# Product five read from its PSUM bank, ones products read a unit later, and distances counted in streamed columns, in an encoder block on one core

## The chip, the cores and the metric

The kernel runs on one core of a Trainium2 chip. The metric is the device time of one launch in microseconds, lower is better. Names of the engines: PE is TensorE's matmul (PEld its weight load), DVE is VectorE, ACT is ScalarE, POOL is GpSimd, SP is SyncE, which issues the DMAs.

## What is computed

One layer of a hybrid encoder block on x of 1024 tokens by 1024 channels, float32:

```python
u = rms_norm(x, norm1_g)
q, k, v, cB, cC, cH, gates = split(u @ w_in)            # 512 each, gates 2048
A = neighbourhood_attention(q, k, v, rpb)               # 8 heads of 64
B = cB * conv3(cC * cH)
m = sigmoid(gA) * (A @ w_attn_branch) + sigmoid(gB) * (B @ w_conv_branch)
x = x + m @ w_o
x = x + square(relu(rms_norm(x, norm2_g) @ w_mlp_in)) @ w_mlp_out   # 1024 -> 4096 -> 1024
```

## The kernel before

**Arithmetic.** Every float32 operand of a product is scaled by a power of two and split into a high and a low float16 half. A product then runs three passes on PE: high by high, high by low, low by high. The power of two comes from a sum of squares (or a maximum) over the weights. Each partition's share is written into a column next to a tile of ones, a matmul with the ones ("ones product", `all_sum`, line 177) adds them over the partitions, DVE reads the result from PSUM (line 180), and `pow2_half` turns it into the scale (lines 401 to 408).

**Seven products.** The gate projection, W1 and W2 use a seven-product scheme for 2 x 2 blocks (`seven`, line 993). Of each weight group two blocks and four sums of blocks are formed. Each product is a *unit* (line 183): 12 matmuls of 512 columns, four row tiles by three passes, into one PSUM bank. The order in W1 is 1, 6, 5, 4, 2, 7, 3; in the gates it is 1, 6, 2, 4, 5, 7, 3. After a unit has been issued, the *post* of the unit before it runs: it reads PSUM and combines products. There are eight PSUM banks that are handed out in turn (`anybank`, line 74), so a bank that is read late holds up the unit that wants it next.

**Posts of W1** (`quad`, line 1282). Product 1 is copied by ACT, products 6 and 2 are added to it by DVE. `post5` (line 1292) copies product 5 to SBUF on ACT (L1293) and subtracts on DVE (L1294). `post7` (line 1296) makes three sums (L1297 to L1299); L1299 uses the copy of product 5. `post3` (L1302) adds product 3 and starts `h_done` (line 1265): ACT's ReLU (L1267) and its square with a sum (L1269), POOL's four sums (L1136), and the store of the seven forms to DRAM (L1273).

**How the work interleaves.** Every engine works its queue in the order in which the program issues it. The program has a foreground list `fg` and a background list `bg` of generators; `unit` lets each of them advance a fixed number of steps (2 and 5 in W1) after its matmuls. `apart(mark, n)` (line 159) keeps a generator waiting until n units have been issued since the mark. So the distance between the issue of a sum and of the ones product that reads it is written in units, whatever their size.

**Weight groups of W1.** There are 16 groups q; group q is used by quad q. `sums1(q)` (line 1190) scales the rows (`rows_scaled`, L941, ACT, eight pieces), takes the sums of squares (`forms_sum`, L950, ACT) and the four sums of blocks (L955, POOL), and adds the two partial sums (`sum_of`, L921 and L922, DVE). `prep1(q)` (line 1204) waits in `gate(q)` until quad q-3 is issued, calls `scale_of` (line 925: the distance, the ones product, the power of two), splits the seven forms with ACT (L974) and DVE (L968) in `forms_split`, and goes on to `sums1(q+1)`. The operands of three groups can be in SBUF at a time. The sums of blocks stand in `tsum`, two groups to a tile of the pool "ws".

**The gates** use the same helpers in `prep_s` (line 978) and `gate_units` (line 1016), where product 5 is copied by ACT as well (line 1047) and read by lines 1031 and 1032. **The projections** (Q, K, conv) get their scale in `Chunk.prep`, through the same `all_sum`; their splits are L287 (ACT) and L275 (DVE), and at the start of the kernel they share the engines with the forms of the tokens (L477 POOL, L479 and L471 ACT, L481 DVE).

**From W1 to W2.** `first2` is put on the background list behind `prep1(15)`: it loads four tiles of W2 (`w2x`) and the first of the stored forms. `prep2(s)` (line 1346) takes squares of W2 (L1359, ACT), `sum_of`, `scale_of`, and then splits activations (L1383 ACT, L1385 DVE) and weights (L1388 ACT, L1392 DVE) for each product; POOL makes the next weight sums (L1398, L1399). Quads 14 and 15 run beside this, then the 28 products of W2.

Of the kernel before, what the change touches and what calls it, by code (L numbers as in the profile page):

```python
# [14 lines left out]
AF = mybir.ActivationFunctionType  # L15
OP = mybir.AluOpType
# [36 lines left out]
def encoder_block(ctx: ExitStack, tc: tile.TileContext, x, weights, cols, gqk, rel, masks, out):  # L53
# [12 lines left out]
    def bank(tag):  # L66
        return psum.tile([128, 512], F32, name="ps_" + tag, tag=tag, bufs=banks[tag])
# [6 lines left out]
    def anybank():  # L74
        rc[0] += 1
        return bank("dsodsods"[rc[0] % 8])
# [78 lines left out]
        forced[0] = False  # L155

    late, units, forced, side = [], [0], [False], [False]

    def apart(mark, n=3):
        while units[0] < mark + n and not forced[0]:  # L160
            yield WAIT

    def built(*chs):
# [10 lines left out]
        turn[0] = (turn[0] + 1) % 4  # L174
        return ones[:, 128 + turn[0]:129 + turn[0]]

    def all_sum(a, out, bk, floor):
        T.matmul(bk[:, 0:1], ones[:, 0:128], a, start=True, stop=True)
        yield
        V.tensor_scalar(sc[:, out], bk[:, 0:1], floor, None, op0=OP.max)  # L180
        yield

    def unit(mms, post=None, steps=0, ticks=0):

        for ps, l, r, a, b in mms:
            T.matmul(ps, l, r, start=a, stop=b)  # L186
        units[0] += 1
        settle()
        if post:
            late.append(post)  # L190
        for i in range(max(steps, ticks)):
            if i < steps:
                step()
            if i < ticks:
                tick()

    def settle():
        while late:
            late.pop(0)()
# [17 lines left out]
    class Chunk:  # L217
# [75 lines left out]
        def largest(self, rm, a, b):  # L293
            o = 0
            for p, (k, w) in enumerate(self.widths):
                while len(self.raw) <= p:
                    yield WAIT
                V.tensor_reduce(sc[:, at(rm, o, k)], self.raw[p][:, :k * w].rearrange("p (k w) -> p k w", k=k),
                                axis=AX, op=OP.max, apply_absolute_value=True)
                o += k  # L300
                yield
            while not self.ready:
                yield WAIT
            mul(rm, self.rows, rm)
            yield
            V.tensor_reduce(sc[:, a], sc[:, rm], axis=AX, op=OP.max, apply_absolute_value=True)
            c = ones_col()
            V.tensor_copy(c, sc[:, a])
            if self.kind != "V":
                yield from apart(units[0], {"A": 3, "B": 3, "O": 1}[self.kind])  # L310
            yield from all_sum(c, b, bank(self.bank) if self.bank else anybank(), 1e-30)

    def push(*chunks):
        for ch in chunks:
# [226 lines left out]
    for p in range(11):  # L541
# [7 lines left out]
        for q in (p,) if p < 6 else (2 * p - 6, 2 * p - 5):  # L549
            c = q // 2 + 3  # L550
# [367 lines left out]
    def sum_of(sm):  # L918

        b, a = cols_of("prep", 1), ones_col()  # L920
        V.tensor_reduce(sc[:, b], sc[:, sm], axis=AX, op=OP.add)  # L921
        V.tensor_copy(a, sc[:, b])  # L922
        return a, units[0]

    def scale_of(am, more):

        a, mark = am
        yield from apart(mark)
        b, s, inv = cols_of("prep", 1), cols_of("prep", 1), keep()
        yield from all_sum(a, b, anybank(), 1e-36)  # L930
        yield from pow2_half(b, 14, s, inv, more)
        return s, inv
# [8 lines left out]
                A.activation(v, v, AF.Copy, scale=sc[:, at(g, 4 * i + k)])  # L941
            yield

    def forms_sum(ch, t):

        sm = cols_of("prep", 2)
        for i in range(2):
            while len(ch.raw) <= i:
                yield WAIT
            A.activation(t[:, 2:4].rearrange("p a c -> p (a c)"), ch.raw[i], AF.Square, accum_out=sc[:, at(sm, i)])  # L950
            yield
        ch.r = [ch.raw[i].rearrange("p (n m) -> p n m", n=2) for i in range(2)]
        (w11, w12), (w21, w22) = ([r[:, 0], r[:, 1]] for r in ch.r)
        for o, a, b in ((0, w11, w12), (1, w12, w22), (2, t[:, 0], w22), (3, t[:, 2], w21)):
            G.tensor_tensor(t[:, o], a, b, op=OP.add)  # L955
        yield
        ch.sum = sum_of(sm)
        yield

# [18 lines left out]
    def prep_s(n):  # L978

        ch = cS[n]  # L980
        t = w3p.tile([128, 4, 512], F32, name="gsum", bufs=1)
        yield from rows_scaled(ch, g1)
        yield from forms_sum(ch, t)
        s, ch.inv = yield from scale_of(ch.sum, 9)
        while done[0] < ch.first:
            yield WAIT
        ch.P = wsp.tile([128, 7, 2, 512], F16, name="w16_s", tag="ws")
        yield from forms_split(ch, t, s, ch.P)
        ch.split = True
# [26 lines left out]
    def gate_units(n, tail=None):  # L1016

        sg = w3p.tile([128, 4, 512], F32, name="sg")
        z = [sg[:, i] for i in range(4)]
        if n == 0:  # L1020
            for g in range(2):
                for half in range(2):
                    ps = anybank()
                    unit(ch_mms(ps, actU, half, cG, 8, 256, 128 * g),
                         lambda ps=ps, g=g, half=half: A.activation(z[2 * half + g], ps, AF.Sigmoid,
                                                                    scale=sc[:, cG.inv]), 3, 4)
            return sg

        def post7(ps):
            V.tensor_tensor(z[2], ps[7], z[1], op=OP.add)  # L1030
            V.tensor_tensor(z[1], z[3], z[1], op=OP.subtract)
            V.tensor_tensor(z[3], z[3], z[2], op=OP.subtract)
            V.tensor_tensor(z[2], ps[4], z[2], op=OP.add)
            if tail:
                A.activation(sg[:, 2:], sg[:, 2:], AF.Sigmoid, scale=sc[:, cS[n].inv])
                tail(sg, 1)

        def post3(ps):
            V.tensor_tensor(z[1], ps[3], z[1], op=OP.add)
            c = 2 if tail else 4  # L1040
            A.activation(sg[:, :c], sg[:, :c], AF.Sigmoid, scale=sc[:, cS[n].inv])
            if tail:
                tail(sg, 0)
        seven(cS[n].P, actS, 0, 512, {
            1: lambda ps: A.activation(z[0], ps[1], AF.Copy),
            6: lambda ps: V.tensor_tensor(z[1], ps[6], z[0], op=OP.add),
            5: lambda ps: A.activation(z[3], ps[5], AF.Copy),
            2: lambda ps: V.tensor_tensor(z[0], ps[2], z[0], op=OP.add),
            7: post7, 3: post3}, 2, 4 if n < 7 else 6, (1, 6, 2, 4, 5, 7, 3))
        return sg  # L1050

# [138 lines left out]
    def sums1(q):  # L1190

        ch = c1[q]
        while q == 2 and pair_done[0] < 4:
            yield
        if q == 0:
            tsum[0] = U2[1][:, 2].rearrange("p s k t -> p (s k t)").bitcast(F32).rearrange("p (i c) -> p i c", i=4)
        elif q == 1 or q % 2 == 0:
            t = wsp.tile([128, 2, 4, 512], F32, name="tsum", tag="ws")
            for i in range(2):
                tsum[q + i] = t[:, i]  # L1200
        yield from rows_scaled(ch, g2)
        yield from forms_sum(ch, tsum[q])

    def prep1(q):

        ch = c1[q]
        yield from gate(q)
        s, ch.inv = yield from scale_of(ch.sum, 9)
        pool, tag = TAGS[q % 3]
        P = P1[q] = pool.tile([128, 7, 2, 512], F16, name="w16_1", tag=tag)  # L1210
        yield from forms_split(ch, tsum[q], s, P)
        ready.add(q)
        if 0 < q < 15:
            yield from sums1(q + 1)
# [67 lines left out]
    def quad(q, c0=0, c1=512):  # L1282
        need(q)
        if c0 == 0:
            while q - 2 in live:
                step()
            live.add(q)
            AS[q] = w4p.tile([128, 7, 512], F32, name="as", tag="as")
        ps = {}
        z = [AS[q][:, i, c0:c1] for i in range(7)]  # L1290

        def post5(ps):
            A.activation(z[3], ps[5], AF.Copy)  # L1293
            V.tensor_tensor(z[1], z[3], z[5], op=OP.subtract)  # L1294

        def post7(ps):
            V.tensor_tensor(z[6], ps[7], z[5], op=OP.add)  # L1297
            V.tensor_tensor(z[2], ps[4], z[6], op=OP.add)  # L1298
            V.tensor_tensor(z[3], z[3], z[6], op=OP.subtract)  # L1299

        def post3(ps):
            V.tensor_tensor(z[1], ps[3], z[1], op=OP.add)  # L1302
            if c1 == 512:
                fg.append(h_done(q))
        seven(P1[q], actU2, c0, c1, {
            1: lambda ps: A.activation(z[4], ps[1], AF.Copy),
            6: lambda ps: V.tensor_tensor(z[5], ps[6], z[4], op=OP.add),
            5: post5,
            2: lambda ps: V.tensor_tensor(z[0], ps[2], z[4], op=OP.add),  # L1309
            7: post7, 3: post3}, 2, 5)  # L1310
# [251 lines left out]
```

## Time and profile before

| | before |
|---|---|
| median of 3 runs | 1300.35 us (1298.75 to 1300.73) |
| profiled execution, time | 1300.49 us |
| profiled execution, span | 1298.7 us |
| mean granted TensorE clock | 0.984 |
| DMA traffic | 173.35 MB, 133 GB/s over the span |

The profile is one execution with the time of every instruction. Lines like `839.94 1.92 ACT as L1267` give the start in microseconds, the duration, the engine, the tile and the line of the kernel. In the timeline a bracket such as `[4.23 <-DVE ones L922]` is the idle time of that engine before the instruction and what ended it. In a table by stage, the columns are the stretch, then the busy time and the count of instructions of PE, PEld, DVE, ACT and POOL, then the granted clock, the DMA share and GB/s. Groups of instructions read `line engine operation out<-in shapes xcount | busy us, mean ns | idle before, and what ended it`.

The stages by time: projections and attention up to about 365 us, gates and branches to 580, the output product to 660, the first norm and quads of the MLP to 720, the rest of W1 to 985, W2 to the end.

### The profile page before, as it was taken

To read this page: it belongs to the slowest core of one execution; us is meant where nothing else is said; L and a number is where in the kernel's file an instruction comes from. 1 tells how busy PE (TensorE), PEld (TensorE's weight loads), DVE (VectorE), ACT (ScalarE), POOL (GpSimd) and SP (SyncE) were. 2 spreads that over 40 slices of the span, in tenths; PEclk is the share of its full clock that TensorE was granted. 3 is DMA by queue.
4 is the path that set the end of the run, shared out by engine and by line. 5 is a ranking of instruction groups with operands and counts; after the bars stand their busy time and mean duration, and the time that the engine had idled before them with its cause. 6 is when DMAs were issued, how large, how long until landed. Compare 5 with 4: busy or idle time off the path is not lost. (4 is left out here: it accounts for less than half of the span.)

```text
span 1298.7 us, 17029 instructions
## 1 busy us (share of the span) xinstructions
PE 1215.0 (94%) x6294; PEld 578.9 (45%) x6294; DVE 946.1 (73%) x1719; ACT 775.1 (60%) x1194; POOL 439.5 (34%) x269
## 2 busy tenths in 40 slices
PE   4999999888999999999987899999998799999998
PEld 3544444444444444444456344444443344444443
DVE  6678867877548877866666666676656688888897
ACT  5777567766455554433677777677664664646430
POOL 2430011121221111101014776686637316080562
PEclk8999999999999999999998899999999899999999
DMA  6557535645662121133474443453382752526212
GB/s 246 122 203 160 115 61 127 143 89 115 129 142 66 52 79 40 59 120 140 89 146 97 171 164 125 158 173 126 147 275 65 273 229 96 228 98 243 80 50 98
DMA packets 170803, 173.35 MB, mean 133 GB/s; under 512 B 131424, under 2 KB 131936, under 8 KB 166624
## 3 DMA queue, kind: packets, MB, share of 16 engines
q1 hardware_dynamic: 170720, 172.27, 44.8%
q8 instruction: 49, 0.80, 0.3%
q14 instruction: 34, 0.28, 0.1%
HBM read 102.51 MB, written 37.75 MB: 108 GB/s over the span
## 5 line engine op out<-in xcount | busy, mean ns | idle before, releaser
L186 PEld LDWEIGHTS <-w 128*128 128x128 f16 x1512 | 148.5, 99 | 171.1 <-issue 25.5
L186 PEld LDWEIGHTS <-ops 128*128 128x128 f16 x1356 | 133.5, 99 | 175.3 <-issue 22.3
L1136 POOL TENSOR_TENSOR as<-as 128x512 f32<-128x512 f32 x64 | 109.2, 1705 | 97.3 <-ACT as L1269 93.6
L851 PE MATMUL ps_d<-uT,w_ws 128*128 128x512 f16 x528 | 127.0, 382 | 2.2 <-ACT w_ws L287 2.2
L186 PE MATMUL ps_s<-ops 128*128 128x512 f16 (+1 forms) x528 | 121.6, 382 | 5.5 <-issue 3.5
L186 PE MATMUL ps_d<-ops 128*128 128x512 f16 x492 | 112.9, 379 | 0.0
L186 PEld LDWEIGHTS <-uT 128*128 128x128 f16 x648 | 64.6, 100 | 68.4 <-issue 3.5
L1383 ACT ACTIVATE ops<-hf,sc 128x2048 f16<-128x2048 f32 x26 | 51.9, 1997 | 67.0 <-PE ps_d L186 25.1
L186 PEld LDWEIGHTS <-w_s 128*128 128x128 f16 x588 | 56.9, 98 | 68.7 <-DVE w_s L968 0.4
L186 PE MATMUL ps_d<-u2T,w 128*128 128x512 f16 (+1 forms) x396 | 84.5, 363 | 2.3 <-DVE as L1298 2.3
L186 PE MATMUL ps_o<-ops 128*128 128x512 f16 x336 | 79.5, 387 | 7.2 <-DVE ops L1392 4.8
L968 DVE SCALAR_TENSOR_TENSOR w<-raw,sc,w 128x512 f16<-128x512 f32 (+1 forms) x32 | 41.8, 1306 | 60.2 <-ACT w L974 60.2
L1267 ACT ACTIVATE as<-as 128x2048 f32<-128x2048 f32 x16 | 30.6, 1910 | 81.6 <-DVE as L1302 81.6
L1385 DVE SCALAR_TENSOR_TENSOR ops<-hf,sc,ops 128x2048 f16<-128x2048 f32 x26 | 70.3, 2702 | 12.1 <-ACT ops L1383 12.1
L955 POOL TENSOR_TENSOR tsum<-raw 128x512 f32<-128x512 f32 x30 | 51.5, 1734 | 75.6 <-ACT raw L941 75.6
L851 PEld LDWEIGHTS <-w_ws 128*128 128x128 f16 x528 | 50.9, 98 | 57.1 <-ACT w_ws L287 2.7
L941 ACT ACTIVATE raw<-raw,sc 128x256 f32<-128x256 f32 x184 | 75.7, 496 | 0.0
L1398 POOL TENSOR_TENSOR raw<-raw 128x1024 f32<-128x1024 f32 x8 | 24.8, 3098 | 142.2 <-DVE ops L1392 142.2
L955 POOL TENSOR_TENSOR gsum<-raw 128x512 f32<-128x512 f32 x14 | 18.7, 1336 | 133.5 <-ACT raw L941 118.8
L968 DVE SCALAR_TENSOR_TENSOR w<-tsum,sc,w 128x1024 f16<-128x1024 f32 x30 | 57.1, 1904 | 0.0
L186 PE MATMUL ps_d<-u2x,w 128*128 128x512 f16 (+1 forms) x228 | 51.0, 379 | 4.7 <-DMA u2x<-v 2.0
L275 DVE SCALAR_TENSOR_TENSOR w_ws<-raw,sc,w_ws 128x512 f16<-128x512 f32 (+2 forms) x72 | 51.4, 767 | 2.6 <-ACT w_ws L287 2.6
(297 smaller groups left out, 2593.7 us busy)
## 6 DMA issues: line engine op xcount, KB each, us to landing
raw<-in_weights SPq DMA_DIRECT2D x92, 512.0 KB, 3.7
hs<-as SPq DMA_DIRECT2D x16, 1792.0 KB, 6.6
hf<-hs SPq DMA_DIRECT2D x26, 1024.0 KB, 9.6
w2x<-in_weights SPq DMA_DIRECT2D x16, 512.0 KB, 7.9
raw<-in_weights SPq DMA_DIRECT2D x16, 384.0 KB, 3.4
xt<-in_x SPq DMA_DIRECT2D x8, 512.0 KB, 10.1
gs<-s SPq DMA_DIRECT2D x4, 1024.0 KB, 5.9
x<-in_x SPq DMA_DIRECT2D x8, 512.0 KB, 8.6
```

The source lines that it names most:

```text
L186: T.matmul(ps, l, r, start=a, stop=b)
L275: V.scalar_tensor_tensor(lo, self.raw[p][:, o:o + m], sc[:, c:c + 1], hi, op0=OP.mult, op1=OP.subtract)
L851: T.matmul(ps, l, r, start=a, stop=b)
L941: A.activation(v, v, AF.Copy, scale=sc[:, at(g, 4 * i + k)])
L955: G.tensor_tensor(t[:, o], a, b, op=OP.add)
L968: V.scalar_tensor_tensor(P[:, a:b, 1], w, sc[:, s], P[:, a:b, 0], op0=OP.mult, op1=OP.subtract)
L1136: sub.tensor_tensor(z[o], z[a], z[b], op=op)
L1267: A.activation(f[:, 0:4], f[:, 0:4], AF.Relu)
L1383: A.activation(P[:, 1, 0], hf, AF.Copy, scale=sc[:, Rs])
L1385: V.scalar_tensor_tensor(P[:, 1, 1], hf, sc[:, Rs], P[:, 1, 0], op0=OP.mult, op1=OP.subtract)
L1398: G.tensor_tensor(w11[i2], w11[i2], w12[i2], op=OP.add)
```

## The change

Five things change together.

- `post5` and the gates' product 5 lose the copy by ACT; DVE's two readers take the PSUM bank.
- `all_sum` has a parameter `lag`: DVE's read of the ones product is issued a unit after the matmul (chunk V excepted, with lag 0).
- A counter `work` adds up the columns that the units stream. `sum_of` returns it, `scale_of` waits n x 6144 columns (6144 are a unit of 12 matmuls of 512), and `forms_sum` waits `gap` x 6144 columns between POOL's sums and the sum of squares.
- In `prep1` the call of `scale_of` stands ahead of `gate(q)`, with n = 1; in `prep_s` n = 2 and gap = 2; in `sums1` gap = 3 from q = 2 on.
- The tiles `tsum` are allocated for groups (1, 2), (3, 4) and so on in place of (1, 2), (2, 3), (4, 5): at odd q.

```diff
--- before.py
+++ after.py
@@ -155,9 +155,10 @@
         forced[0] = False
 
     late, units, forced, side = [], [0], [False], [False]
-
-    def apart(mark, n=3):
-        while units[0] < mark + n and not forced[0]:
+    work = [0]
+
+    def apart(mark, n=3, of=units):
+        while of[0] < mark + n and not forced[0]:
             yield WAIT
 
     def built(*chs):
@@ -174,9 +175,10 @@
         turn[0] = (turn[0] + 1) % 4
         return ones[:, 128 + turn[0]:129 + turn[0]]
 
-    def all_sum(a, out, bk, floor):
+    def all_sum(a, out, bk, floor, lag=1):
         T.matmul(bk[:, 0:1], ones[:, 0:128], a, start=True, stop=True)
         yield
+        yield from apart(units[0], lag)
         V.tensor_scalar(sc[:, out], bk[:, 0:1], floor, None, op0=OP.max)
         yield
 
@@ -185,6 +187,7 @@
         for ps, l, r, a, b in mms:
             T.matmul(ps, l, r, start=a, stop=b)
         units[0] += 1
+        work[0] += len(mms) * mms[0][0].shape[-1]
         settle()
         if post:
             late.append(post)
@@ -308,7 +311,7 @@
             V.tensor_copy(c, sc[:, a])
             if self.kind != "V":
                 yield from apart(units[0], {"A": 3, "B": 3, "O": 1}[self.kind])
-            yield from all_sum(c, b, bank(self.bank) if self.bank else anybank(), 1e-30)
+            yield from all_sum(c, b, bank(self.bank) if self.bank else anybank(), 1e-30, self.kind != "V")
 
     def push(*chunks):
         for ch in chunks:
@@ -920,12 +923,12 @@
         b, a = cols_of("prep", 1), ones_col()
         V.tensor_reduce(sc[:, b], sc[:, sm], axis=AX, op=OP.add)
         V.tensor_copy(a, sc[:, b])
-        return a, units[0]
-
-    def scale_of(am, more):
+        return a, work[0]
+
+    def scale_of(am, more, n=3):
 
         a, mark = am
-        yield from apart(mark)
+        yield from apart(mark, n * 6144, work)
         b, s, inv = cols_of("prep", 1), cols_of("prep", 1), keep()
         yield from all_sum(a, b, anybank(), 1e-36)
         yield from pow2_half(b, 14, s, inv, more)
@@ -941,7 +944,7 @@
                 A.activation(v, v, AF.Copy, scale=sc[:, at(g, 4 * i + k)])
             yield
 
-    def forms_sum(ch, t):
+    def forms_sum(ch, t, gap):
 
         sm = cols_of("prep", 2)
         for i in range(2):
@@ -953,7 +956,7 @@
         (w11, w12), (w21, w22) = ([r[:, 0], r[:, 1]] for r in ch.r)
         for o, a, b in ((0, w11, w12), (1, w12, w22), (2, t[:, 0], w22), (3, t[:, 2], w21)):
             G.tensor_tensor(t[:, o], a, b, op=OP.add)
-        yield
+        yield from apart(work[0], gap * 6144, work)
         ch.sum = sum_of(sm)
         yield
 
@@ -980,8 +983,8 @@
         ch = cS[n]
         t = w3p.tile([128, 4, 512], F32, name="gsum", bufs=1)
         yield from rows_scaled(ch, g1)
-        yield from forms_sum(ch, t)
-        s, ch.inv = yield from scale_of(ch.sum, 9)
+        yield from forms_sum(ch, t, 2)
+        s, ch.inv = yield from scale_of(ch.sum, 9, 2)
         while done[0] < ch.first:
             yield WAIT
         ch.P = wsp.tile([128, 7, 2, 512], F16, name="w16_s", tag="ws")
@@ -1028,8 +1031,8 @@
 
         def post7(ps):
             V.tensor_tensor(z[2], ps[7], z[1], op=OP.add)
-            V.tensor_tensor(z[1], z[3], z[1], op=OP.subtract)
-            V.tensor_tensor(z[3], z[3], z[2], op=OP.subtract)
+            V.tensor_tensor(z[1], ps[5], z[1], op=OP.subtract)
+            V.tensor_tensor(z[3], ps[5], z[2], op=OP.subtract)
             V.tensor_tensor(z[2], ps[4], z[2], op=OP.add)
             if tail:
                 A.activation(sg[:, 2:], sg[:, 2:], AF.Sigmoid, scale=sc[:, cS[n].inv])
@@ -1044,7 +1047,6 @@
         seven(cS[n].P, actS, 0, 512, {
             1: lambda ps: A.activation(z[0], ps[1], AF.Copy),
             6: lambda ps: V.tensor_tensor(z[1], ps[6], z[0], op=OP.add),
-            5: lambda ps: A.activation(z[3], ps[5], AF.Copy),
             2: lambda ps: V.tensor_tensor(z[0], ps[2], z[0], op=OP.add),
             7: post7, 3: post3}, 2, 4 if n < 7 else 6, (1, 6, 2, 4, 5, 7, 3))
         return sg
@@ -1194,18 +1196,18 @@
             yield
         if q == 0:
             tsum[0] = U2[1][:, 2].rearrange("p s k t -> p (s k t)").bitcast(F32).rearrange("p (i c) -> p i c", i=4)
-        elif q == 1 or q % 2 == 0:
+        elif q % 2:
             t = wsp.tile([128, 2, 4, 512], F32, name="tsum", tag="ws")
             for i in range(2):
                 tsum[q + i] = t[:, i]
         yield from rows_scaled(ch, g2)
-        yield from forms_sum(ch, tsum[q])
+        yield from forms_sum(ch, tsum[q], 3 if q > 1 else 2)
 
     def prep1(q):
 
         ch = c1[q]
+        s, ch.inv = yield from scale_of(ch.sum, 9, 1)
         yield from gate(q)
-        s, ch.inv = yield from scale_of(ch.sum, 9)
         pool, tag = TAGS[q % 3]
         P = P1[q] = pool.tile([128, 7, 2, 512], F16, name="w16_1", tag=tag)
         yield from forms_split(ch, tsum[q], s, P)
@@ -1290,13 +1292,12 @@
         z = [AS[q][:, i, c0:c1] for i in range(7)]
 
         def post5(ps):
-            A.activation(z[3], ps[5], AF.Copy)
-            V.tensor_tensor(z[1], z[3], z[5], op=OP.subtract)
+            V.tensor_tensor(z[1], ps[5], z[5], op=OP.subtract)
 
         def post7(ps):
             V.tensor_tensor(z[6], ps[7], z[5], op=OP.add)
             V.tensor_tensor(z[2], ps[4], z[6], op=OP.add)
-            V.tensor_tensor(z[3], z[3], z[6], op=OP.subtract)
+            V.tensor_tensor(z[3], ps[5], z[6], op=OP.subtract)
 
         def post3(ps):
             V.tensor_tensor(z[1], ps[3], z[1], op=OP.add)
```

## The prediction

> **What bounds the kernel now.** I read the busy shares first, then the shares stage by stage, the chain of waits, the timeline of one stretch of the MLP's first half, and last the starts of TensorE's units. The page:
>
> ```profile
> span 1298.7 us, 17029 instructions
> ## 1 busy us (share of the span) xinstructions
> PE 1215.0 (94%) x6294; PEld 578.9 (45%) x6294; DVE 946.1 (73%) x1719; ACT 775.1 (60%) x1194; POOL 439.5 (34%) x269
> ```
>
> TensorE (PE) is the bound on average, and 1298.7 - 1215.0 = 83.7 us of the span is all that a reordering can win. The busy time by stage says where that lies:
>
> ```profile
> 365.00:580.00 215.00, 215.00 (x1011) 97.50 (x1010) 166.88 (x329) 107.56 (x169) 31.34 (x24) 1.00 0.25 72
> ...
> 720.00:955.00 235.00, 225.63 (x1038) 101.29 (x1038) 157.21 (x249) 165.75 (x243) 159.88 (x96) 0.99 0.45 154
> 955.00:1035.00 80.00, 68.76 (x300) 30.08 (x299) 45.01 (x43) 47.96 (x49) 41.55 (x20) 0.94 0.56 200
> ```
>
> The gates (365 to 580) are full: 215.00 of 215.00. The W1 products (720 to 955) lose 9.4 us, the passage to W2 (955 to 1035) 11.2. How a W1 quad loses time shows in its units, PE alone:
>
> ```profile
> 714.85 2.75 PE L186 MATMUL ps_d<-u2T,w 128*128 128x512 f16 x12
> 721.84 0.16 PE L178 MATMUL ps_s<-ones 128*128 128x1 bf16 x1 [4.23 <-DVE ones L922]
> 721.86 5.22 PE L186 MATMUL ps_d<-u2x,w 128*128 128x512 f16 x12
> 726.91 2.75 PE L186 MATMUL ps_s<-u2T,w 128*128 128x512 f16 x12
> 729.50 2.75 PE L186 MATMUL ps_o<-u2T,w 128*128 128x512 f16 x12
> ...
> 739.86 0.38 PE L186 MATMUL ps_d<-u2T,w 128*128 128x512 f16 x1
> ...
> 948.54 2.75 PE L186 MATMUL ps_d<-u2T,w 128*128 128x512 f16 x12
> ```
>
> A unit starts 729.50 - 726.91 = 2.59 us after the one before, so the 7 units of a quad take 18.13 us, 18.16 with the ones product. Quad 2 starts at 714.85, quad 3 at 739.86, quad 14 at 948.54. Twelve quads took 233.69 us instead of 12 x 18.16 = 217.9: **15.8 us lost**. Of this 25.01 - 18.16 = 6.85 us lie in quad 2, and 8.9 in the eleven behind it, 0.8 each. The chain shows what holds those:
>
> ```profile
> 839.94 1.92 ACT as L1267
> 841.93 1.86 issue
> 844.46 3.73 ACT w L974 x4
> 848.19 3.19 ACT raw L941 x8
> 854.12 1.31 DVE as L1294
> 859.53 1.92 ACT as L1267
> ```
>
> It doesn't touch PE. From one L1267 to the next, 859.53 - 839.94 = 19.59 us here, runs a circle of two in-order queues. ACT does ReLU and square (L1267, L1269), four splits (L974), eight row scalings (L941), two sums of squares (L950), and only then the copy of product 5 (L1293). DVE waits for that copy, and behind it in DVE's queue stand the sums of the next weights (L921, L922) and the rest of the quad's adds, whose last (L1302) lets the next L1267 go. The timeline of the same quad:
>
> ```profile
> 853.51 0.58 ACT L1293 ACTIVATE as<-ps_s 128x512 f32<-128x512 f32 x1
> 854.12 1.31 DVE L1294 TENSOR_TENSOR as<-as 128x512 f32<-128x512 f32 x1 [1.60 <-ACT as L1293]
> ...
> 855.99 0.16 PE L178 MATMUL ps_s<-ones 128*128 128x1 bf16 x1 [1.09 <-DVE sc L110]
> ...
> 859.53 1.91 ACT L1267 ACTIVATE as<-as 128x2048 f32<-128x2048 f32 x1 [5.44 <-DVE as L1302]
> ```
>
> PE feels the circle only through the ones product in its own queue, 1.09 us late here.
>
> **The change, part by part.**
>
> *Product 5 read from its bank.* ACT loses L1293, and the readers of its copy, L1294 and L1299, take a PSUM operand as L1297 does. Grouped by line, 720 to 955:
>
> ```profile
> L1294 DVE TENSOR_TENSOR as<-as 128x512 f32<-128x512 f32 x12 | 15.0, 1254 | 17.6 <-ACT as L1293 17.6
> ...
> L1299 DVE TENSOR_TENSOR as<-as 128x512 f32<-128x512 f32 x12 | 10.2, 848 | 0.0
> ...
> L1297 DVE TENSOR_TENSOR as<-ps_s,as 128x512 f32<-128x512 f32 x12 | 8.2, 680 | 0.0
> L1302 DVE TENSOR_TENSOR as<-ps_o,as 128x512 f32<-128x512 f32 x12 | 8.2, 680 | 0.0
> L1307 DVE TENSOR_TENSOR as<-ps_d,as 128x512 f32<-128x512 f32 x12 | 8.1, 677 | 0.0
> L1293 ACT ACTIVATE as<-ps_s 128x512 f32<-128x512 f32 x12 | 6.9, 577 | 0.0
> ```
>
> Per quad ACT gains 0.58 us, and DVE (1254 - 680) + (848 - 680) = 0.74 us. More than that, L1294 no longer stands behind ACT's L950. The circle becomes: L1267 to the end of the second L950 as now, 853.51 + 0.1 - 839.94 = 13.67 us, then L921 and L922 (0.35), and the four adds that remain (4 x 0.68 = 2.72, some already past), about 3.1: **16.8 us**, below PE's 18.16. From then on PE sets the pace.
>
> [...] The rows differ: 680 ns from the bank against 848 and 1254 from SBUF beside POOL's work, and the measurement decides.
>
> The bank is now held until L1299 and not until the copy. Product 5 of the next quad reuses it 18 us later, while L1299 runs one unit after product 7: slack of some 10 us, no cost in W1. The same edit in the gates costs nothing at best and wins nothing, because PE never waits there. If it did cost there, the bound is its two adds, 7 x 2 x 0.01; I take 0.
>
> *Ones products and distances.* In W1 the sum of squares of weight group q is now read three units of streamed columns after POOL's sums are issued, and its ones product goes out ahead of the gate, that is before quad q-1, where it went out after the first unit of quad q-2. The sum is then ready some 3 us before PE comes to it, and the 4.23 us of quad 2 with the half-speed unit behind it (5.22 instead of 2.75) go as well. So **quads 2 to 13: -15.8 us**. Bounds: -6.85 (quad 2 alone, the circle staying) and -15.8 (nothing is left).
>
> The price is in the lead. The whole split of group q (L974, L968) now runs in quad q-1 and not in q-2: it ends some 5 us before PE wants it instead of 23. Inside W1 that is enough. Two places feel it.
>
> *Q.* The maximum after the ones product is read a unit later, also for chunk Q at the start. Its splits fall behind the activation sums of the next token tile:
>
> ```profile
> 66.61 2.29 DVE L481 TENSOR_TENSOR s<-sform,s 128x2048 f16<-128x2048 f32 x1 [0.74 <-ACT s L479]
> 68.82 1.41 DVE L275 SCALAR_TENSOR_TENSOR w_ws<-raw,sc,w_ws 128x512 f16<-128x512 f32 x2
> 70.53 6.40 DVE L275 SCALAR_TENSOR_TENSOR w_ws<-raw,sc,w_ws 128x512 f16<-128x512 f32 x4 [0.30 <-ACT w_ws L287]
> ```
> ```profile
> 76.99 0.59 PE L186 MATMUL ps_d<-w_ws,uT 128*128 128x512 f16 x2 [0.87 <-DVE w_ws L275]
> ```
>
> PE already waits here for the last L275, which ends at 76.93. That end moves by one more L481 (2.29) ahead of it: **+2.3 us**, bounds 0.5 and 4.
>
> *Entry to W1.* A ones stall of about 4 us at 686 to 690 goes, but PE's next wait is for transposes that arrive at 692 and 696, so nothing is won. Product 4 of quad 1's first half then waits for L1299 of quad 0, about +1: **+1.0**, bounds -1 and 3.
>
> *Passage to W2.* Here the lost lead is paid once.
>
> ```profile
> w2x<-in_weights SPq DMA_DIRECT2D x16, 512.0 KB, 7.9
> ```
> ```profile
> 948.65 4.32 SPq L207 DMA_DIRECT2D w2x<-in_weights  x4
> ...
> 962.72 2.00 ACT L1359 ACTIVATE h<-w2x,sc 128x2048 bf16<-128x2048 f32 x1
> ...
> 966.98 0.16 DVE L921 TENSOR_REDUCE sc<-sc 128x1 f32<-128x6 f32 x1 [4.15 <-ACT h L1359]
> ...
> 981.27 3.33 POOL L1398 TENSOR_TENSOR raw<-raw 128x1024 f32<-128x1024 f32 x1 [3.42 <-DVE ops L1392]
> ...
> 985.53 2.75 PE L186 MATMUL ps_o<-ops 128*128 128x512 f16 x12
> ...
> 999.54 4.44 PE L186 MATMUL ps_s<-ops 128*128 128x512 f16 x12 [3.48 <-issue]
> ```
>
> Measured from quad 14's start (948.54): the loads of w2x go out at 0.1, once group 15 is split. After the change that split ends in quad 14 itself, at about 12.5. With the page's 7.9 us from issue to landing, and 1.9 for the issues ahead, the pair that L1359 reads is there at 22.3; its two halves (4.2 us up to 966.9) end near 26.5 instead of 18.3, and L921 with them. Behind L921 in DVE's queue stand quad 14's last adds, and product 5's bank now hangs on one of these: the third unit of quad 15 starts near 29.1 instead of 23.3, 5.8 us idle with a half-speed unit (+2.4) behind it. From L921 to W2's first unit it was 985.53 - 966.98 = 18.6 us, 15.4 of it until the operand was ready (33.8); with one unit (2.4) more before the ones product is read, it is ready at 44.3, and W2 starts at 44.6 instead of 37.0. POOL's sums (L1398 and L1399, 13.7 us) shift by the same, and the second operand comes at about 60 where its first unit started at 51.0. But before's own waits behind that (3.48 at 999.54 with its slow unit, and two more up to 1024) are partly swallowed: the third operand's first unit ends near 78 where it was 75.4, and the fourth adds 2.2. **+5.0**, bounds 1 and 10.
>
> [...]
>
> **Sum.** 1300.49 (the profiled execution; its span is 1298.7, the median of the runs shown 1300.35) - 15.8 + 2.3 + 1.0 + 5.0 = **1293.0 us**.
>
> **Rivals.**
> - *The passage costs nothing*: W2's start had waits of its own (3.48 and its slow unit), and w2x may land earlier. Then 1300.49 - 15.8 + 2.3 + 1.0 = 1288.0. For it: POOL stood idle before L1398. Against: L921 was already the last thing awaited there.
> - *The circle stays.* L921 stands behind the second L950 in both, and the late adds behind L921. If the sum is issued before the columns are streamed, L1302 is as late as now and only quad 2 gains: 1300.49 - 6.85 + 8.3 = 1301.9, no difference to be seen. Against: 16.8 leaves 1.3 us.
> - *Slower: the lost quad of lead is exposed whole* at W2's first operands. They depend on w2x loads that leave 12.4 us later, on the sum behind them and on L1383 behind ACT's queue; if nothing overlaps, PE stands for a quad (18.16) in place of 5: 1300.49 - 15.8 + 3.3 + 18.2 = 1306.2. It decides from the point at which the passage costs over 12.5 us, that is, when W2's first units start 12.5 us later than 985.53 relative to quad 14. Against: the chain above gives 7.6.
>
> **How the numbers follow.** Forecast 0.47 (1290 to 1297); passage free 0.20 (1286 to 1290); circle stays 0.16 (1297 to 1303); slower 0.17 (1303 to 1310). The range 1286.5 to 1304 leaves out some 2 in 10, mostly the slower end. A measurement of this kernel can tell about 0.2% from no change, 2.6 us: faster is below 1297.75, slower above 1302.95. Faster 0.68 (forecast, passage free and a hundredth of the rest), same 0.15, slower 0.17.
>
> **What would show it.** Starts of quads 3 to 14 exactly 18.16 apart and no wait at their ones products show the circle broken; L1294 and L1299 at about 680 ns the bank read. A first Q unit near 79.7 shows the Q stall. An L921 behind L1359 some 26 us into quad 14, an idle PE in quad 15 and W2 44 us after quad 14's start show the passage. Quads still 19 apart with PE waiting for L922, or W2 later than 49, prove me wrong.

## The result, and the profile after

The changed kernel takes 1303.95 us (median of 11 runs, 1302.50 to 1305.36) against 1300.39 us before (11 runs). The ratio is 1.0029, 95% interval 1.0019 to 1.0038: **a little slower**, where 1293.0 us and faster had been forecast. The profiled execution has a span of 1302.2 us against 1298.7.

The busy time of each engine on the page after, and the busy time by stage in the same columns as before:

```profile
## 1 busy us (share of the span) xinstructions
PE 1220.6 (94%) x6294; PEld 580.2 (45%) x6294; DVE 933.8 (72%) x1719; ACT 763.3 (59%) x1169; POOL 436.5 (34%) x269
```
```profile
365.00:580.00 215.00, 210.61 (x981) 94.93 (x979) 154.97 (x320) 100.09 (x158) 36.52 (x25) 0.99 0.24 65
...
720.00:955.00 235.00, 230.63 (x1078) 104.65 (x1077) 157.37 (x261) 173.11 (x251) 163.82 (x104) 0.99 0.46 158
955.00:1035.00 80.00, 63.09 (x273) 27.21 (x272) 37.65 (x42) 38.95 (x40) 38.99 (x18) 0.91 0.55 195
```

DVE and ACT are relieved by 12 us each, and W1 loses 4.4 us instead of 9.4. But the gates, full before, now lose 4.4, and the passage to W2 loses 16.9 instead of 11.2. A fixed window hides that everything has shifted, so I also counted PE's matmuls (without the ones products) and took the start of the same one in every trace: number 2100 (in the gates' second group), 3050 (in the output product), 3716 (first of quad 2), 4724 (first of quad 14), 5100 (in W2) and the last, 6247. The differences between these starts are the stages, in us:

| | to 2100 | gates | entry to W1 | quads 2 to 13 | passage | rest of W2 |
|---|---|---|---|---|---|---|
| before | 382.1 | 205.4 | 127.4 | 233.7 | 97.0 | 249.2 |
| after | 383.9 | 211.6 | 127.5 | 222.4 | 103.9 | 249.0 |
| difference | +1.8 | +6.2 | +0.1 | -11.3 | +6.9 | -0.2 |

They add up to +3.5 us, which is the difference of the spans. **The gain in W1 came; the gates and the passage gave more than all of it back.**

*W1.* The add that used to wait for ACT, and the one that used to read the copy, grouped by line, 720 to 955:

```profile
L1295 DVE TENSOR_TENSOR as<-ps_d,as 128x512 f32<-128x512 f32 x12 | 8.3, 692 | 1.3
...
L1300 DVE TENSOR_TENSOR as<-ps_d,as 128x512 f32<-128x512 f32 x12 | 8.2, 680 | 0.0
```

L1295 (L1294 before) takes 692 ns instead of 1254 and waits 1.3 us in all instead of 17.6; L1300 takes 680 instead of 848. PE's timeline, by which quads 2, 3 and 4 start at 722.92, 743.98 and 763.77, and quad 14 at 945.32:

```profile
722.90 0.16 PE L179 MATMUL ps_o<-ones 128*128 128x1 bf16 x1 [1.63 <-DVE ones L925]
722.92 2.75 PE L188 MATMUL ps_d<-u2T,w 128*128 128x512 f16 x12
...
743.96 0.16 PE L179 MATMUL ps_o<-ones 128*128 128x1 bf16 x1 [2.75 <-DVE ones L925]
743.98 4.38 PE L188 MATMUL ps_d<-u2T,w 128*128 128x512 f16 x12
...
763.74 0.17 PE L179 MATMUL ps_o<-ones 128*128 128x1 bf16 x1
763.77 1.46 PE L188 MATMUL ps_d<-u2T,w 128*128 128x512 f16 x6
...
945.29 0.17 PE L179 MATMUL ps_o<-ones 128*128 128x1 bf16 x1
945.32 2.75 PE L188 MATMUL ps_d<-u2T,w 128*128 128x512 f16 x12
```

From quad 4 on there is no wait: ten quads in 945.32 - 763.77 = 181.55 us, 18.16 each. But the ones product ahead of quad 3 waits 2.75 us, and the unit behind it runs 4.38 us instead of 2.75, with a granted clock of 0.62 from 743.90 to 748.40.

*The gates.* Timeline of SP, DVE and PE around the only large wait:

```profile
377.22 10.36 SPq L916 DMA_TRANSPOSE uT<-gs  x8
...
387.68 1.47 SPq L210 DMA_DIRECT2D raw<-in_weights  x3
...
393.32 1.22 DVE L301 TENSOR_REDUCE sc<-raw 128x4 f32<-128x1024 f32 x1 [8.96 <-DMA raw<-in_weights]
...
395.30 0.16 PE L179 MATMUL ps_d<-ones 128*128 128x1 bf16 x1 [3.67 <-DVE ones L311]
395.32 4.44 PE L188 MATMUL ps_s<-qD,w_s 128*128 128x512 f16 x12
```

PE stands in front of the ones product of the next branch weights. DVE has waited 8.96 us for those weights: their loads left SP at 387.68, behind a train of eight transposes. The same stretch before:

```profile
372.57 10.53 SPq L913 DMA_TRANSPOSE uT<-gs  x8
383.20 14.05 SPq L207 DMA_DIRECT2D raw<-in_weights  x4
```

There the train went 4.6 us earlier, while PE's units here were only 1.4 us earlier (376.02 against 377.45 for the first product of this group).

The delay begins ahead of the gates. Timeline of SP before and after, where the first trains of transposes start:

```profile
334.75 2.31 SPq L207 DMA_DIRECT2D raw<-in_weights  x2
...
338.45 22.93 SPq L913 DMA_TRANSPOSE qD<-gs  x16
```
```profile
343.89 0.33 SPq L210 DMA_DIRECT2D raw<-in_weights  x1
344.27 21.74 SPq L916 DMA_TRANSPOSE qD<-gs  x16
```

The transposes start 5.8 us later. They stand behind a load into a tile whose weights must have been split first. These are the weights of the first gates' group, which get their scale as the projections do, in `Chunk.prep`, now with the lag. In the traces their ones product is 1.4 us later than before (313.96 against 312.56), DVE's read of it 2.6 us (320.32 against 317.70), and the end of their last split 7.2 us (343.86 against 336.71). The load leaves right behind that.

*The passage.* SP's queue, ACT and PE in the timeline after:

```profile
954.81 2.66 SPq L210 DMA_DIRECT2D w2x<-in_weights  x4
...
959.26 24.71 SPq L1275 DMA_DIRECT2D hs<-as  x2
...
984.06 0.61 SPq L1377 DMA_DIRECT2D ops<-hs  x1
...
994.94 2.00 ACT L1384 ACTIVATE ops<-ops,sc 128x2048 f16<-128x2048 f32 x1 [14.88 <-DMA ops<-hs]
...
1000.62 0.58 PE L188 MATMUL ps_s<-ops 128*128 128x512 f16 x1 [7.05 <-ACT ops L1389]
...
1016.54 4.36 SPq L1343 DMA_DIRECT2D hf<-hs  x4
...
1028.24 2.00 ACT L1384 ACTIVATE ops<-hf,sc 128x2048 f16<-128x2048 f32 x1 [14.21 <-DMA hf<-hs]
...
1032.94 0.59 PE L188 MATMUL ps_s<-ops 128*128 128x512 f16 x1 [6.86 <-ACT acc L1483]
```

PE waits 7.05 us for the second product and 6.86 us for the fourth. Both times ACT waits for a load of a stored form. The first of these loads (L1377) leaves at 984.06, right behind the store of quad 14's forms (the second of the two in the row of 959.26), which had been held in SP's queue until POOL's sums were done (the last of them ends at 983.43). In SP's queue before, the load stood ahead of that store:

```profile
966.87 0.33 SPq L1376 DMA_DIRECT2D ops<-hs  x1
...
998.66 0.53 SPq L1273 DMA_DIRECT2D hs<-as  x1
```

The load for the fourth product (the first in the row of 1016.54) stands behind quad 15's store in both kernels; it left 63.6 us after the start of quad 14 before, and leaves 71.2 us after it now.

### The profile page after: what moved, and what is told of

Same layout as the page of the kernel before. It is cut to its first block, busy times and chain, and to the rows that moved or that the text cites. A ratio compares the mean times of both kernels' runs of the same rounds, so it can differ in the third digit from the quotient of the medians.

```text
span 1302.2 us, 17008 instructions
## 1 busy us (share of the span) xinstructions
PE 1220.6 (94%) x6294; PEld 580.2 (45%) x6294; DVE 933.8 (72%) x1719; ACT 763.3 (59%) x1169; POOL 436.5 (34%) x269
## 4 chain that ended last, share of the span: by engine, by line
PE 61%; DVE 13%; issue 8%; ACT 7%; DMA 7%; POOL 4%; SPq 1%; DVEq 0%; POOLq 0%; ACTq 0%
PE ps_d L188 22%; PE ps_s L188 19%; PE ps_o L188 13%; PE ps_d L854 4%; DVE w_ws L278 1%; DMA PT<-P 1%; DMA u2x<-v 1%; POOL as L1138 1%; DMA xt<-in_x 1%; DVE ops L1393 1%; DVE P L818 1%; DVE sz L792 1%; ACT w L977 1%; POOL sform L480 1%; DMA hf<-hs 1%
## 5 line engine op out<-in xcount | busy, mean ns | idle before, releaser
L188 PE MATMUL ps_s<-ops 128*128 128x512 f16 (+1 forms) x528 | 123.1, 384 | 17.6 <-ACT ops L1389 7.0
L188 PE MATMUL ps_d<-u2T,w 128*128 128x512 f16 (+1 forms) x420 | 90.1, 367 | 3.2 <-DMA u2T<-v 2.8
L188 PE MATMUL ps_s<-u2x,w 128*128 128x512 f16 (+1 forms) x396 | 84.5, 364 | 2.1 <-DMA u2x<-v 2.0
L971 DVE SCALAR_TENSOR_TENSOR w<-tsum,sc,w 128x1024 f16<-128x1024 f32 x30 | 61.4, 2087 | 0.0
```

What stands on the lines that cost most here:

```text
L971: V.scalar_tensor_tensor(P[:, a:b, 1], w, sc[:, s], P[:, a:b, 0], op0=OP.mult, op1=OP.subtract)
```

## The experiments

The theory after this: the bank read alone breaks the circle of ACT and DVE; the losses come from the new distances. The rival: the later ones products free W1, and the bank read does little. The kernels and their stages, counted as above (the stages are those of the profiled execution, which lies up to 4.0 us from the median: in run 3 it was the fastest, 3.8 us below):

| | time, us | ratio to before, 95% | to 2100 | gates | entry | quads 2-13 | passage |
|---|---|---|---|---|---|---|---|
| bank alone | 1279.93 | 0.9849 (0.9830 to 0.9869) | 381.3 | 205.4 | 123.8 | 223.8 | 92.5 |
| distances alone | 1320.52 | 1.0152 (1.0127 to 1.0176) | 382.8 | 213.5 | 128.5 | 235.3 | 106.3 |
| no lag | 1297.71 | 0.9984 (0.9965 to 1.0004) | 381.1 | 207.2 | 129.4 | 218.9 | 103.8 |
| stores by POOL | 1320.17 | 1.0158 (1.0138 to 1.0178) | 385.0 | 211.7 | 127.4 | 238.1 | 104.7 |
| W1's distances undone | 1342.69 | 1.0315 (1.0292 to 1.0339) | 383.0 | 211.5 | 124.8 | 264.3 | 103.8 |
| bank, W1's distances | 1295.03 | 0.9964 (0.9948 to 0.9979) | 380.9 | 205.4 | 129.4 | 219.1 | 104.8 |
| gap one | 1368.68 | 1.0527 (1.0505 to 1.0549) | 383.3 | 211.9 | 135.2 | 290.2 | 97.2 |
| form loads by ACT | 1292.74 | 0.9939 (0.9924 to 0.9954) | 383.2 | 211.2 | 127.3 | 222.3 | 91.2 |
| bank, gates' distances | 1288.74 | 0.9924 (0.9909 to 0.9939) | 381.3 | 207.9 | 128.0 | 224.5 | 92.5 |
| bank, lag | 1343.87 | 1.0341 (1.0313 to 1.0369) | 384.3 | 213.9 | 124.7 | 264.6 | 103.5 |
| gates without lag | 1305.21 | 1.0052 (1.0033 to 1.0070) | 383.2 | 213.2 | 127.2 | 222.3 | 103.3 |
| bank, form loads by ACT | 1274.74 | 0.9819 (0.9801 to 0.9837) | 383.6 | 205.4 | 123.7 | 223.8 | 85.7 |

**1. The bank read alone.** The kernel before with

```diff
-            A.activation(z[3], ps[5], AF.Copy)
-            V.tensor_tensor(z[1], z[3], z[5], op=OP.subtract)
+            V.tensor_tensor(z[1], ps[5], z[5], op=OP.subtract)
...
-            V.tensor_tensor(z[3], z[3], z[6], op=OP.subtract)
+            V.tensor_tensor(z[3], ps[5], z[6], op=OP.subtract)
```

and the same in the gates.

> The kernel before, with one part of the change: product 5 is read from its bank in W1 and in the gates; all distances as before. Theory A (the bank read breaks the circle of ACT and DVE, and the losses of the change come from its new distances): quads 3 to 14 start 18.2 us apart instead of 19.0, some 9 us gained in the eleven quads, the 4.23 us wait in quad 2 shorter, nothing lost in the gates and the passage: 1289 to 1293 us. Theory B (the later ones products free W1, the bank read alone does nothing): 1299 to 1301 us with quads still 19 apart.

1279.93 us, a larger gain than expected: the quads gained 9.9 us, the entry 3.6, the passage 4.5, and the gates lost nothing. Quads 3 to 13 take 18.15 or 18.16 us each, so the circle is broken by this edit alone; the 5.9 us that are left over 12 x 18.16 lie in quad 2, which takes 24.10. The timeline of one quad (the add of product 5 is L1292 in this kernel):

```profile
838.77 0.68 DVE L1292 TENSOR_TENSOR as<-ps_s,as 128x512 f32<-128x512 f32 x1
...
839.97 0.16 DVE L921 TENSOR_REDUCE sc<-sc 128x1 f32<-128x2 f32 x1 [0.27 <-ACT tsum L950]
...
846.09 0.17 PE L178 MATMUL ps_s<-ones 128*128 128x1 bf16 x1
```

The add is done before ACT has finished its second L950, DVE idles only 0.27 us for ACT before the sum, and the ones product waits for nothing.

**2. The distances alone.** The changed kernel with the copy put back (the reverse of the edit above).

> The changed kernel with the copy of product 5 put back: the distances alone. Theory A: the circle is back at over 19 us a quad, so the eleven quads cost some 9 to 11 us more than in the changed kernel while all of its losses stay: 1311 to 1315 us. Theory B: the same time as the changed kernel, 1303 to 1305 us.

1320.52 us, above the range that was expected. The quads take 235.3 us again, 1.6 more than before, although every ones product comes a unit or more later. DVE waits for the copy as it did:

```profile
880.17 0.58 ACT L1296 ACTIVATE as<-ps_d 128x512 f32<-128x512 f32 x1
880.78 1.30 DVE L1297 TENSOR_TENSOR as<-as 128x512 f32<-128x512 f32 x1 [1.01 <-ACT as L1296]
...
883.00 0.16 PE L179 MATMUL ps_o<-ones 128*128 128x1 bf16 x1 [0.57 <-DVE ones L925]
```

The rival falls: the bank read is what frees W1.

**3. No lag.** The changed kernel with

```diff
-    def all_sum(a, out, bk, floor, lag=1):
+    def all_sum(a, out, bk, floor, lag=0):
...
-            yield from all_sum(c, b, bank(self.bank) if self.bank else anybank(), 1e-30, self.kind != "V")
+            yield from all_sum(c, b, bank(self.bank) if self.bank else anybank(), 1e-30)
```

> The changed kernel with lag 0: the maximum after a ones product is read at once again, all else as changed. Theory A1 (the unit's lag moves the splits, and with them the loads of weights in SP's queue, behind PE): the wait of 3.83 us at the gates' first branch weights falls below 1.5 us without a slow unit (-4), the first Q unit comes 2 us earlier: 1297 to 1299 us. Rival A2 (the wait in the gates comes from the distances in columns in the gates' own preparation): the gates still stall, 1301 to 1303 us.

1297.71 us, not to be told from before; its runs spread from 1293.88 to 1301.58. From V's last products to the second unit of Q it is 12.27 us (64.53 to 76.80), as before (65.17 to 77.42), and 13.86 in the changed kernel (64.63 to 78.49): the Q term is the lag's. In the gates 4.4 of the 6.2 us go, and the quads take 218.9 us instead of 222.4: without the lag quad 2 takes 18.28 us and quad 3 18.15.

**4. Stores by POOL.**

```diff
-        SP.dma_start(HS[q // 4][:, :, q % 4], f)
+        G.dma_start(HS[q // 4][:, :, q % 4], f)
```

> The changed kernel with the stores of W1's forms issued by GpSimd behind its own sums instead of by SP. Theory A (in the passage to W2, PE's waits of 7.05 and 6.86 us come from loads of the forms that stand in SP's queue behind stores which wait for GpSimd's sums): both waits go or fall below 3 us, 1293 to 1297 us. Rival (GpSimd's weight sums for the second and fourth products are late themselves): the waits stay, 1302 to 1305 us.

1320.17 us, slower for a reason that neither theory had. The store now stands in POOL's queue behind the weight sums of the next group, and the tile that it reads comes free later. ACT waits for it with the copy of product 1, and the splits stand behind that:

```profile
893.25 0.60 ACT L1307 ACTIVATE as<-ps_d 128x512 f32<-128x512 f32 x1 [2.87 <-DMA hs<-as]
```

Most quads are about 19.5 us apart. In the passage PE's waits before the second and the fourth product fall to 2.14 and 3.64 us, as the theory has it, but a wait of 8.06 us at W2's ones product comes instead.

**5. W1's distances undone.** In the changed kernel

```diff
-        s, ch.inv = yield from scale_of(ch.sum, 9, 1)
         yield from gate(q)
+        s, ch.inv = yield from scale_of(ch.sum, 9)
...
-        yield from forms_sum(ch, tsum[q], 3 if q > 1 else 2)
+        yield from forms_sum(ch, tsum[q], 0)
```

with the tiles of the sums allocated as before.

> The changed kernel with W1's distances as before (scale behind the gate and three units after the sum, no distance ahead of the sum, the sums' tiles as before); the bank read, the lag and the gates' distances stay. Up to the output product the changed kernel lies 8.3 us behind the run with the bank read alone (+6.3 against -2.0 us, each against before), and from there to the end some 14 us. Theory: W1's distances cost those 14 us, in quad 3 and in the passage: 1287 to 1290 us, the passage without the two 7 us waits, the gates' wait of 3.83 us still there. Rival (the passage is late because the bank is held or because of the lag): 1298 to 1303 us.

1342.69 us: the expectation failed by over 50 us. The quads are 22 us apart. Run 10 says why.

**6. The bank read and W1's distances.** In the changed kernel lag 0 as in run 3, and

```diff
-        yield from forms_sum(ch, t, 2)
-        s, ch.inv = yield from scale_of(ch.sum, 9, 2)
+        yield from forms_sum(ch, t, 0)
+        s, ch.inv = yield from scale_of(ch.sum, 9)
```

> The bank read and W1's distances; lag 0 and the gates' distances as before. Theory: 14 us more than the bank read alone, 1292 to 1296 us, with quad 14 split late (the loads of w2x 9 to 12 us after quad 14 starts), and nothing lost up to the output product. Rival (the lag is what costs the lead in W1): 1280 to 1285 us.

1295.03 us, 15 more than the bank read alone. The quads are 4.7 us *better* (219.1; 12 x 18.16 would be 217.9): quad 2 takes 18.15 us instead of 24.10, so without the lag W1's distances gain there by themselves. The entry costs 5.6 and the passage 12.3.

**7. Gap one.** In the changed kernel

```diff
-        yield from forms_sum(ch, tsum[q], 3 if q > 1 else 2)
+        yield from forms_sum(ch, tsum[q], 1)
```

> The changed kernel with W1's distance ahead of the sum cut from 3 units (2 for the first groups) to 1. Theory (split, row scaling, sums, 3 units, 1 unit and the lag close a circle of the seven units of a quad, so that the lead lost at the start is never won back): with two units less the lead grows by two units a quad until the gate stops it; the loads of w2x leave at the start of quad 14, the passage costs what it did before or less: 1289 to 1294 us. Rival (the lead is lost by the scale's place, or again in each quad): 1301 to 1305 us.

1368.68 us, the worst of all. My picture of a lead that can be won back by shorter distances was wrong. With the sum and the ones product issued sooner, PE comes to the ones product before ACT has done the squares, and waits 4.36 us in ten of the quads:

```profile
820.96 0.16 PE L179 MATMUL ps_d<-ones 128*128 128x1 bf16 x1 [4.36 <-DVE ones L925]
```

With the lag, three units of distance give 222.4 us of quads, one unit 290.2, and the old distances 264.3 (run 5); two units weren't run.

**8. Form loads by ACT.** In the changed kernel

```diff
-                SP.dma_start(later["h", 1], HS[0][:, ORDER[1][0]])
+                A.dma_start(later["h", 1], HS[0][:, ORDER[1][0]])
...
-        SP.dma_start(later["h", n], HS[s][:, f])
+        (A if n < 7 else SP).dma_start(later["h", n], HS[s][:, f])
```

> The changed kernel with the loads of the first seven W2 products' stored forms issued by ScalarE and not by SP, so that they don't stand behind the stores that wait for GpSimd's sums. Theory: PE's waits of 7.05 us (second product) and 6.86 us (fourth product) fall below 3 us, 1293 to 1298 us. Rival (GpSimd's weight sums, or ScalarE held up by its own DMA issues, set the same time): 1302 to 1306 us.

1292.74 us, 11 less than the change. The passage takes 91.2 us instead of 103.9. The load leaves 7.5 us earlier (1.4 of them because quad 14 starts earlier), while the store still sits in SP's queue, and PE's wait of 7.05 us is gone:

```profile
976.54 0.35 ACTq L1377 DMA_DIRECT2D ops<-hs  x1
...
981.33 2.00 ACT L1384 ACTIVATE ops<-ops,sc 128x2048 f16<-128x2048 f32 x1 [2.60 <-DMA ops<-hs]
982.13 29.25 SPq L1275 DMA_DIRECT2D hs<-as  x2
...
992.08 0.38 PE L188 MATMUL ps_s<-ops 128*128 128x512 f16 x1
```

So the order of SP's queue is worth 12.7 us of the passage here, more than the 6.9 that the change had added; with the bank read alone it is worth 6.8 (run 12).

**9. The bank read and the gates' distances.** The edits of runs 3 and 5 together: lag 0, W1's order and lengths as before; a distance of three units is counted in columns here, which in the half quads of 256 columns is six units.

> The bank read and the gates' distances in columns (two units ahead of the sum, two behind); lag 0 and W1's distances as before. Theory (the gates' distances by themselves move nothing that PE waits for; the lag does): as the bank read alone, 1279 to 1283 us, no wait at the gates' first branch weights. Rival: the wait of some 4 us there, 1284 to 1287 us.

1288.74 us: neither the theory nor, in size, the rival. The gates lose 2.5 us, not at the branch weights but at their own ones product, which waits 2.15 us, and the entry loses 4.2. The first transposes start at 338.51, as before.

**10. The bank read and the lag.** The edits of run 5 and of run 6's diff together: the gates' and W1's distances as before.

> The bank read and the lag alone; the gates' and W1's distances as before. Theory (the lag lengthens the circle of split, sums and ones product by a unit, so that with W1's old distances the ones product of W1 leaves the start of the quad and goes out three units behind a sum that ScalarE hasn't reached): quads over 21 us apart with PE waiting 2 to 3.6 us at each ones product, as with W1's distances undone: 1335 to 1345 us. Rival (that loss came from the gates' distances beside the lag): 1283 to 1290 us.

1343.87 us, as expected. One quad's sum and ones product:

```profile
894.37 0.15 DVE L924 TENSOR_REDUCE sc<-sc 128x1 f32<-128x2 f32 x1 [9.37 <-ACT tsum L953]
...
894.77 0.16 PE L179 MATMUL ps_d<-ones 128*128 128x1 bf16 x1 [3.46 <-DVE ones L925]
```

In the order of the program the ones product stands behind the first unit of a quad without the lag, and behind the fifth with it. ACT then finishes the squares only just before, DVE has waited 9.37 us for them, and PE 3.46. One unit's lag costs 40.8 us of quads here (264.6 against 223.8). W1's distances in the changed kernel make up for the lag but for 3.5 us (222.4 against 218.9 in run 3). In the gates the lag alone costs 8.5 us (213.9 against 205.4).

**11. The gates without lag.** `scale_of` hands a lag on to `all_sum`, and in the changed kernel

```diff
-        s, ch.inv = yield from scale_of(ch.sum, 9, 2)
+        s, ch.inv = yield from scale_of(ch.sum, 9, 2, 0)
```

> The changed kernel with lag 0 in the gates' own scale alone. Theory (the lag makes the gates' splits, and so the loads of the branch weights behind eight transposes in SP's queue, a unit later, and PE comes to their ones product first): the 3.83 us wait and its slow unit go: 4 to 5 us less than the changed kernel, 1298 to 1300 us. Rival (the gates' columns): 1303 to 1305 us.

1305.21 us: the theory falls, the gates don't get better (213.2). The first transposes start at 343.99, about as in the changed kernel (344.27), while they start at 337.74 with no lag anywhere (run 3). So the lag that holds up SP's queue isn't in the scale that this run changes: the rows above put it in the scale of the first gates' group, which keeps its lag here. PE waits 2.70 us at the ones product of the branch weights, 3.67 in the changed kernel (the 3.83 of the expectations is this wait with the 0.16 of the product itself). Then it waits 2.23 us at the gates' own ones product, where run 9 has 2.15.

The gates take 205.4 us with neither lag nor columns (runs 1 and 6), 207.9 with the columns alone (run 9), 213.9 with the lag alone (run 10) and 211.6 with both. So the lag is the larger part, and the two don't add up. No run takes the lag out of the first gates' group's scale alone; that step is read from the rows.

**12. The bank read and the form loads by ACT.** Runs 1 and 8 together.

> A version to beat both: the kernel before with the bank read and with the loads of the first seven W2 products' forms issued by ScalarE. Theory (these loads wait in SP's queue behind stores here as well: ScalarE waits 5.12 and 5.84 us for them with the bank read alone, PE 3.1 us): 1275 to 1279 us. Rival (the waits were covered, ScalarE loses time issuing): 1279 to 1283 us.

**1274.74 us**, ratio 0.9819 (0.9801 to 0.9837): faster than before and after. The passage takes 85.7 us. PE is full in the gates and in W1 (215.00 of 215.00 and 235.00 of 235.00 us) and loses 2.7 us in the stretch of the passage:

```profile
365.00:580.00 215.00, 215.00 (x1011) 97.45 (x1010) 165.59 (x328) 103.11 (x162) 32.16 (x25) 1.00 0.25 71
720.00:955.00 235.00, 235.00 (x1091) 106.17 (x1090) 151.27 (x251) 171.32 (x244) 157.97 (x98) 0.99 0.51 172
955.00:1035.00 80.00, 77.31 (x353) 34.65 (x351) 55.55 (x53) 54.77 (x53) 39.40 (x16) 0.98 0.64 230
```

## Why the prediction was wrong

The forecast was 1293.0 us and faster; the changed kernel is slower. By its steps:

- **The gates, "I take 0": this is the step that failed.** The argument was that PE never waits there, so nothing could be won; it then priced only the two adds and let the lag and the distances go without a price. For the adds it was right (205.4 us in run 1, as before); no run shows the 0.01 us that it put on each as a bound: in the gates they took 692 ns each from SBUF before, and from the bank after L1034 took 691 to 692 and L1035 679 to 680. The lag and the columns cost 6.2 us. A stage without slack is where a later ones product must be priced, not where it is free. The price went by a way that wasn't followed: a unit's lag in the scale of the first gates' group, its splits later, trains of transposes behind them in SP's queue, the loads of the branch weights behind the transposes, and PE in front of their ones product. Run 10 shows that the lag alone costs 8.5 us, run 9 that the columns alone cost 2.5.
- **Quads 2 to 13, -15.8: right in mechanism, too large.** It was -11.3. The circle broke, at 18.16 us a quad, and run 1 shows that the bank read alone does that. The missing 4.5 us lie between the starts of quads 2 and 4: 2.75 us at the ones product ahead of quad 3 and 1.63 in the half-speed unit. I had the sum ready 3 us before PE from the first quad on. Run 3 shows that the lag is what it missed: without it this wait is gone and the quads take 218.9 us.
- **The passage, +5.0: +6.9, but by another chain.** W2's first unit starts 982.10 - 945.32 = 36.8 us after quad 14, not 44.6; before it was 37.0. The w2x loads left at 9.5, not 12.5, and the third unit of quad 15 waited 0.36 us for DVE's adds and not 5.8. What cost was the second and fourth products, by loads of forms behind a store in SP's queue (run 8). The forecast named POOL's sums there. Against the bank read alone the passage loses 11.4 us, and the lag alone (run 10) loses 11.0 there, W1's distances alone (run 6) 12.3.
- **Q, +2.3: right in mechanism, 1.6 by the rows of run 3.** The +1.8 up to matmul 2100 isn't all Q's: run 12, the same program as run 1 up to W2, differs from it there by 2.3 us.
- **Entry, +1.0:** +0.1. The bank read alone gains 3.6 us there (run 1), so the distances cost as much.
- **The gain put on the wrong part.** The forecast gave the -15.8 to the bank read and the distances together. Alone the first is worth -18.5 us and the distances cost 22 (1320.52 - 1298.47). Together that would be +3.5; it was +3.6. That the sum fits so well is chance: in the quads it would be -9.9 + 1.6 = -8.3 and was -11.3, in the gates +8.1 and was +6.2.
- **The slower rival** had a chance of 0.17 and one mechanism, the lead lost whole at the passage. The time came out in its range by chance, for the mechanism didn't: 6.9 us in the passage instead of 18.2, and 6.2 in the gates.
- **The direct read against a copy first:** the measured 692 and 680 ns are 562 and 168 ns less than from SBUF, which decides for the direct read here. The adds from SBUF were slow beside POOL's work: in the trace before, L1299 took 680 ns in the five instances outside it and 1065 on average in the nine beside it, while the adds with a PSUM operand in W1 took 673 to 692 either way.

What stays open: which of the distances makes the entry 4 to 6 us longer than with the bank read alone (runs 6 and 9), and why lag and distances together cost no more in the passage than either alone.

## What to carry to other kernels

A change made of several parts wants a sum for each part alone; here one edit was worth 1.5% and the others cost more than that. Where the order of the work is written as distances in a program, a later reader moves all that hangs on it, the transfers in a shared queue first (here the first transposes left SP 5.8 us later): look at what stands in that queue between the old place and the new one. A stage in which the bounding engine never waits has no room for a moved step, and is the first place to price one: here the gates, full before, lost 6.2 us.

## What the hardware showed

Between waits of 2 and 3.3 us, a wait's length didn't decide whether TensorE came back at half speed. The last products of W2 are preceded by the same idle time of 2.05 us in both kernels, and the unit behind it took 4.44 us before, where the granted clock was 0.50 from 1283.26 to 1286.66 us, and 2.75 after, at a granted clock of 1.00:

```profile
1282.71 4.44 PE L186 MATMUL ps_s<-ops 128*128 128x512 f16 x12 [2.05 <-DVE x L1493]
```
```profile
1287.91 2.75 PE L188 MATMUL ps_s<-ops 128*128 128x512 f16 x12 [2.05 <-DVE x L1494]
```

Of the fourteen traces here, five show 4.41 to 4.44 us at this place and nine 2.75. In the run with the bank read and the lag, two waits of equal length in one trace differ in the same way:

```profile
785.55 0.16 PE L179 MATMUL ps_d<-ones 128*128 128x1 bf16 x1 [3.30 <-DVE ones L925]
785.57 4.44 PE L188 MATMUL ps_s<-u2x,w 128*128 128x512 f16 x12
...
829.26 0.16 PE L179 MATMUL ps_d<-ones 128*128 128x1 bf16 x1 [3.29 <-DVE ones L925]
829.29 2.75 PE L188 MATMUL ps_s<-u2x,w 128*128 128x512 f16 x12
```

The prediction had a half-speed unit behind the wait of 4.23 us in quad 2 (5.22 instead of 2.75 us), and in the same trace stands the shorter wait of 2.05 us, also with a slow unit behind it. So a stall of 2.05 to 3.7 us cost itself and, in some cases, 1.6 to 1.7 us more; what decides that isn't shown.
